# Cosine attention on one core: the order of work on all five engines replaced, the program left as it is

## The chip, the core and the metric

The kernel runs on one core of one Trainium2 chip. The metric is the device time of one execution in microseconds. A core has four compute engines that this kernel uses side by side: TensorE (PE in the profile; it multiplies and transposes), VectorE (DVE), ScalarE (ACT) and GpSimd (POOL); SyncE (SP) issues nearly all transfers. Each engine works through its own list of instructions strictly in order. An instruction that needs a result of another engine waits for a semaphore, and everything behind it on the same engine waits with it.

## The reference

Inputs Q, K and V are 8 x 12 x 512 x 64 floats, tau is 0.1.

```python
Q_norm = Q / (norm(Q, axis=-1) + 1e-10)
K_norm = K / (norm(K, axis=-1) + 1e-10)
scores = einsum('bhqd,bhkd->bhqk', Q_norm, K_norm) / tau
weights = exp(scores - max(scores))
weights = weights / (sum(weights) + 1e-10)
out = einsum('bhqk,bhkd->bhqd', weights, V)
```

Scores lie between -10 and 10, so the kernel leaves the maximum out of the exponent. For 96 heads of 512 x 512 scores that is 25.2 million exponentials.

## The kernel before

**Tiling.** Two heads form a pair, and there are 48 pairs, 0 to 47. Of each pair, 128 partitions hold four query rows (or key rows) each. The work of one pair is a fixed set of operations, which the program names with a kind and the pair's number:

- LD.s.0 and LD.s.1 load Q and K (256 KB each, line 429), LV.s loads V (line 432). SP issues them.
- SQ.s.0 squares Q and K on POOL (line 250). SSQ.s adds the squares in groups on PE (line 268, eight matmuls), and RED.s.0 on DVE sums the rest (line 276).
- NEW.g.0 to NEW.g.7 on DVE turn the sums of a group of one or two pairs into inverse norms, by an integer first guess and two Newton steps (lines 390 to 402). Pairs 0 to 2 take them by a logarithm and an exponential on ACT instead (LN and EX, lines 282 and 286).
- SCL.s.0 (Q, on DVE) and SCL.s.1 (K, mostly on POOL) scale rows to unit length in bf16 (line 296; line 327 for pair 0).
- TR.s transposes both on PE (line 484), EVA.s copies the result out of PSUM on DVE (line 490). For seven pairs K is transposed by a transfer instead, XT.s.1.
- SCO.s.0 to SCO.s.3 are the scores on PE, two matmuls of 512 columns each (line 512; line 359 for pair 0).
- EXP.s.0 to EXP.s.3 are the exponentials on ACT, 128 x 1024 each (line 527; lines 364 and 523 for the first and the last pair).
- VC.s converts V to bf16 on POOL (line 532), beside a column of ones.
- PV.s.h.t multiply weights and V on PE (line 555, four matmuls of 65 columns each); the ones give the sum of the weights. For the last pair they are PV.47.i.c (line 612).
- RCP.s and NRM.s divide on DVE (lines 569 and 571; 626 and 628 for the last pair), ST.s stores (line 575; 632 for the last pair). Of the last pair the output goes in three parts; ACT issues the last store.

**Buffers.** Score banks are two: the scores of a chunk may start once the exponential two chunks earlier has read its bank. Q and K lie in 18 buffers, V in 6 (LV.s waits for VC.(s-6)), squares in 6, the scaled rows and their transposes in 5 each, the weights in 3, outputs in 8. The PSUM banks for transposes, square sums and outputs pass from one user to the next.

**Order.** Nothing is planned when the kernel is built. A table, ORDER, holds one written-out list for each engine, and the program emits each engine's operations in that order:

```python
order = {e: [by_token.pop(t) for t in text.split()] for e, text in ORDER.items()}
```

Waits come from each operation's list of needs; a wait on a semaphore value that the engine has already seen is left out:

```python
for p in o.waits:
    k = id(p.sem)
    if p.val > max(seen.get(k, 0), want.get(k, (None, 0))[1]):
        want[k] = (p.sem, p.val)
```

A list therefore decides two things: when an operation gets its turn, and which operations stand behind it while it waits. The lists hold 200 operations for SP, 143 for POOL, 451 for DVE, 702 for PE and 212 for ACT.

Of the kernel before, what the change touches and what calls it, by code (L numbers as in the profile page):

```python
# [124 lines left out]
def bass_cosine_similarity_attention_kernel(  # L125
# [518 lines left out]
    if FILL[1]:  # L644
# [8 lines left out]
XT = {9: (1,), 15: (1,), 21: (1,), 27: (1,), 33: (1,), 39: (1,), 45: (1,)}  # L653
# [15 lines left out]
        LD.0.0.0 LD.0.0.1 LD.1.0 LD.1.1 LD.2.0 LD.2.1 LD.3.0 LD.3.1 LV.0 LD.4.0 LD.4.1 LD.5.0 LD.5.1 LD.6.0 LV.1  # L669
        LD.6.1 LD.7.0 LD.7.1 LD.9.1 LD.9.0 LV.2 LV.3 LV.5 LD.8.1 LD.8.0 LV.4 LD.13.0 LD.15.0 LV.7 LD.11.1 LD.10.0  # L670
        LD.10.1 LD.11.0 LV.6 LV.8 LD.16.0 LD.14.1 ST.1 LD.12.0 LD.12.1 LD.13.1 LD.15.1 ST.4 XT.9.1 LD.18.0 LV.9
        LD.14.0 LV.10 LD.21.0 ST.0 LD.17.0 LV.14 LV.11 LD.16.1 LD.19.0 ST.5 ST.3 LD.24.0 LD.17.1 ST.2 LV.12 LV.15
        LD.18.1 LD.27.0 ST.6 LD.20.0 LV.13 LD.19.1 LD.23.0 LD.20.1 XT.15.1 LV.17 LV.16 LD.21.1 LD.24.1 LD.23.1 ST.7
        LD.22.0 LD.27.1 LV.20 ST.9 LD.30.0 LD.22.1 LV.21 LV.18 LD.25.0 LD.26.0 ST.8 LV.23 LD.25.1 ST.10 LD.28.0 LV.19
        LD.26.1 LD.29.0 LD.31.0 LD.31.1 LD.28.1 XT.21.1 LD.35.0 ST.11 ST.13 LD.32.0 LV.22 ST.12 LD.35.1 LV.25 ST.14
        LD.40.0 LD.29.1 ST.16 LD.30.1 LV.24 ST.19 LD.33.0 LD.36.0 LD.40.1 ST.15 LD.32.1 LD.33.1 LV.26 LV.27 LD.44.0
        ST.17 LV.28 XT.27.1 ST.20 LD.42.0 ST.23 LV.29 ST.18 LD.39.1 LD.34.1 LD.34.0 LD.37.1 LD.41.0 LV.32 LD.37.0
        LD.42.1 ST.22 LV.33 LD.36.1 LV.31 LV.30 ST.21 LD.39.0 ST.25 LD.38.0 LD.47.0 LV.35 ST.24 LV.34 XT.33.1 LD.38.1
        LV.37 LV.38 ST.28 ST.29 LD.44.1 LV.36 LD.45.1 LD.41.1 LD.43.0 LV.43 LD.46.0 LD.43.1 ST.26 ST.27 LD.45.0 LV.41
        LV.42 LV.44 ST.30 LV.40 ST.33 ST.32 XT.39.1 LV.39 LD.46.1 LD.47.1 ST.31 ST.36 LV.45 ST.37 LV.47 ST.38 ST.34  # L680
# [13 lines left out]
        wz RED.0.0.0 RED.0.1.0 RED.0.1.1 SCL.0.1.0 SCL.0.0.0 RED.0.0.1 EVA.0.1.0 SCL.0.1.1 EVA.0.0.0 SQ.1.1 SCL.0.0.1
        EVA.0.1.1 RED.1.0 EVA.0.0.1 SCL.1.1 SCL.1.0 RED.2.0 EVA.1.1 EVA.1.0 SCL.2.0 SCL.2.1 RED.3.0 NEW.0.0 NEW.0.1
        NEW.0.2 EVA.2 NEW.0.3 NEW.0.4 NEW.0.5 NEW.0.7 NEW.0.6 SCL.3.1 RED.4.0 SCL.3.0 RCP.0 NEW.1.0 NRM.0 RED.5.0
        NEW.1.1 NEW.1.2 NEW.2.0 EVA.3 NEW.1.3 NEW.2.1 NEW.1.4 NEW.2.2 NEW.1.5 NEW.1.6 NEW.1.7 SCL.4.0 RED.6.0 NEW.2.3
        RCP.1 NEW.2.4 NRM.1 RED.7.0 NEW.2.5 NEW.2.6 NEW.3.0 EVA.4 NEW.3.1 SCL.5.0 NEW.2.7 NEW.3.2 RCP.2 NRM.2 RED.9.0
        NEW.3.3 NEW.3.4 EVA.5 NEW.3.5 NEW.3.7 NEW.3.6 SCL.6.0 RCP.3 NRM.3 RED.8.0 NEW.4.0 NEW.4.1 EVA.6 SCL.7.0
        NEW.4.2 NEW.4.3 RCP.4 NEW.4.4 NRM.4 NEW.4.5 NEW.4.6 EVA.7 NEW.4.7 SCL.8.0 RCP.5 NRM.5 RED.10.0 SCL.9.0 EVA.8  # L700
        EVA.9 RED.11.0 NEW.5.0 NEW.5.1 NEW.5.2 RCP.6 NRM.6 NEW.5.3 NEW.5.4 RED.13.0 NEW.5.5 NEW.5.7 NEW.5.6 SCL.10.0
        RCP.7 NRM.7 RED.12.0 SCL.11.0 EVA.10 NEW.6.0 NEW.6.1 NEW.6.2 EVA.11 NEW.6.3 NEW.6.4 NEW.6.5 NEW.6.6 NEW.6.7
        RED.15.0 SCL.12.0 RCP.8 NRM.8 RED.14.0 EVA.12 NEW.7.0 NEW.7.1 NEW.7.2 SCL.13.0 NEW.7.3 RCP.9 NRM.9 NEW.7.4
        RED.16.0 NEW.7.5 NEW.7.7 EVA.13 NEW.7.6 SCL.14.0 RCP.10 NRM.10 RED.17.0 SCL.15.0 EVA.14 NEW.8.0 EVA.15 NEW.8.1
        NEW.8.2 NEW.8.3 NEW.8.4 RCP.11 NRM.11 NEW.8.5 NEW.8.6 SCL.17.0 NEW.8.7 SCL.16.0 RED.18.0 RCP.12 NRM.12
# [26 lines left out]
        SCO.1.1 TR.2 PV.0.0.0 PV.0.0.1 PV.0.0.2 SCO.1.2 PV.0.0.3 PV.0.1.0 SCO.1.3 SSQ.4 SCO.2.0 PV.0.1.1 PV.0.1.2  # L732
# [108 lines left out]
```

## Time and profile before

| | |
|---|---|
| three timed runs | 191.36, 192.54 and 193.3 us, median 192.54 us |
| the profiled execution's own time | 191.03 us |
| its span, first to last instruction | 189.2 us |
| busy: ACT, PE, POOL, DVE | 181.3, 174.0, 160.1, 146.1 us |
| transfers | 51.73 MB, mean 273 GB/s |
| clock granted to PE | 1.0 throughout |

The span is what the views show; the 1.83 us between it and the execution's own time lie around it. Busy time of PE is modelled at the ends of matmuls, so its share says less than ACT's. An idle gap of an engine is put down to what released the instruction behind it, by the time of semaphore events. A row of the timeline or of the chain gives the start in us, the length in us, the engine, the line and the operation; neighbours of the same kind are merged, with a count.

### The profile page before, as it was taken

The numbers are of one execution on the slowest core, as the hardware profiler recorded it, in microseconds if no ns is written. First come the engines' busy times: TensorE is split into PE (matmuls) and PEld (weight loads), VectorE is DVE, ScalarE is ACT, GpSimd is POOL, SyncE is SP. The second block draws the span as 40 slices with busy tenths as digits, with TensorE's granted clock in tenths as the row PEclk, the third lists the DMA queues.
The fourth block names the chain that finished last, engine by engine and source line by source line (L and its number), as shares of the span: only waits on it lengthen the run. The fifth ranks groups of instructions, "written<-read, shape, count | busy, mean of one in ns | idle before, by whom it ended". The sixth has DMA issues, their size and how long they took to land.

```text
span 189.2 us, 7234 instructions
## 1 busy us (share of the span) xinstructions
PE 174.0 (92%) x3023; PEld 110.2 (58%) x3023; DVE 146.1 (77%) x451; ACT 181.3 (96%) x209; POOL 160.1 (85%) x147
## 2 busy tenths in 40 slices
PE   7999998999998999998898999999999999988893
PEld 5455664665665565665565656565656666654542
DVE  2999988879887977878798688876869877697424
ACT  5599999999999999999999999999999999999992
POOL 1599999999999999999999999999899998355100
PEclk9999999999999999999999999999999999999999
DMA  5999999579999999999999999999999570938423
GB/s 151 335 349 349 348 350 368 175 234 310 361 359 251 309 353 346 314 254 349 376 373 303 241 343 299 352 255 281 294 318 328 132 243 22 309 90 170 132 93 116
DMA packets 56257, 51.73 MB, mean 273 GB/s; under 512 B 6944, under 2 KB 56224, under 8 KB 56224
## 3 DMA queue, kind: packets, MB, share of 16 engines
q1 hardware_dynamic: 55792, 50.93, 86.4%
q8 instruction: 24, 0.39, 0.9%
q10 hardware_dynamic: 432, 0.33, 0.6%
q14 instruction: 9, 0.07, 0.1%
HBM read 37.75 MB, written 12.58 MB: 266 GB/s over the span
## 4 chain that ended last, share of the span: by engine, by line
ACT 84%; PE 6%; DVE 4%; POOL 2%; DMA 2%; issue 0%; ACTq 0%; DVEq 0%
ACT et L527 80%; ACT et L523 2%; DMA qk<-in_K_dram 2%; PE bps L268 2%; PE scps L512 1%; POOL qn L296 1%; PE scps L359 1%; POOL sq L250 1%; DVE qt L490 1%; PE bps L555 1%; PE bps L484 1%; DVE qn L296 1%; DVE qn L327 1%; ACT et L364 1%; PE bps L333 0%
## 5 line engine op out<-in xcount | busy, mean ns | idle before, releaser
L527 ACT ACTIVATE et<-scps 128x1024 bf16<-128x1024 f32 x184 | 168.9, 1168 | 0.2 <-PE scps L512 0.2
L250 POOL TENSOR_TENSOR sq<-qk 128x1024 bf16<-128x1024 f32 (+2 forms) x48 | 87.3, 1830 | 6.0 <-DMA qk<-in_Q_dram 5.7
L512 PE MATMUL scps<-qt 64*128 64x512 bf16 x376 | 74.1, 386 | 8.5 <-ACT et L527 7.2
L555 PE MATMUL bps<-vb,et 128*128 128x65 bf16 x1472 | 66.4, 194 | 0.0
L555 PEld LDWEIGHTS bps<-vb,et 128*128 128x128 bf16 x1472 | 51.8, 98 | 24.5 <-issue 16.2
L296 POOL TENSOR_TENSOR qn<-qk,rk 128x512 bf16<-128x512 f32 x44 | 45.3, 1042 | 9.4 <-DVE rk L398 5.7
L490 DVE COPY qt<-bps 128x1024 bf16<-128x1024 bf16 (+1 forms) x46 | 29.9, 650 | 10.9 <-PE bps L484 10.0
L296 DVE TENSOR_TENSOR qn<-qk,nps 128x512 bf16<-128x512 f32 x50 | 33.8, 681 | 0.5
L571 DVE TENSOR_TENSOR ob<-bps,rd 128x512 f32<-128x512 f32 x47 | 32.5, 692 | 1.1
L512 PEld LDWEIGHTS scps<-qt 64*128 64x128 bf16 x376 | 18.3, 93 | 25.9 <-ACT et L527 14.3
L268 PE MATMUL bps<-sq,ident 128*128 128x128 bf16 x376 | 29.1, 220 | 0.5 <-POOL qn L296 0.5
L532 POOL TENSOR_SCALAR vb<-vf 128x512 bf16<-128x512 f32 x48 | 29.5, 625 | 0.0
L268 PEld LDWEIGHTS bps<-sq,ident 128*128 128x128 bf16 x376 | 21.1, 98 | 11.0 <-issue 8.1
L569 DVE RECIPROCAL rd<-bps 128x8 f32<-128x8 f32 x47 | 9.7, 207 | 18.7 <-PE bps L555 15.2
L484 PE MATMUL bps<-ident,qn 64*128 64x64 bf16 x680 | 17.9, 191 | 1.4 <-DVE nps L276 0.3
L484 PEld LDWEIGHTS bps<-ident,qn 64*128 64x128 bf16 x680 | 13.2, 95 | 7.8 <-DVE nps L276 3.4
L276 DVE TENSOR_REDUCE nps<-bps 128x16 f32<-128x128 f32 x45 | 13.4, 297 | 2.1 <-PE bps L268 2.1
L390 DVE TENSOR_TENSOR nps<-nps,ys 128x32 f32<-128x32 f32 (+1 forms) x48 | 9.1, 192 | 1.0
L394 DVE SCALAR_TENSOR_TENSOR nps<-nps,ys 128x32 f32<-128x32 f32 (+1 forms) x48 | 9.1, 191 | 0.7
L237 PE MATMUL scps<-warm_in 128*128 128x256 bf16 x23 | 4.8, 394 | 1.1 <-DVE warm_in L232 1.1
L398 DVE SCALAR_TENSOR_TENSOR nps<-nps,ys 128x16 f32<-128x16 f32 (+1 forms) x25 | 4.3, 177 | 0.5
L402 DVE TENSOR_SCALAR ys<-nps 128x32 int32<-128x32 int32 (+1 forms) x24 | 4.4, 181 | 0.4
(45 smaller groups left out, 46.8 us busy)
## 6 DMA issues: line engine op xcount, KB each, us to landing
vf<-in_V_dram SPq DMA_DIRECT2D x48, 256.0 KB, 5.4
qk<-in_Q_dram SPq DMA_DIRECT2D x47, 256.0 KB, 5.9
qk<-in_K_dram SPq DMA_DIRECT2D x47, 256.0 KB, 6.0
out_dram<-ob SPq DMA_DIRECT2D x47, 256.0 KB, 4.5
qk<-in_Q_dram SPq DMA_DIRECT2D x2, 128.0 KB, 2.6
qk<-in_K_dram ACTq DMA_DIRECT2D x2, 128.0 KB, 2.8
out_dram<-ob SPq DMA_DIRECT2D x1, 128.0 KB, 2.3
qt<-qn SPq DMA_TRANSPOSE x7, 3.5
```

Source lines behind the costliest of these rows:

```text
L250: emit = lambda e: e.tensor_tensor(out=b, in0=a, in1=a, op=ALU.mult)
L268: last = e.matmul(out=ps[:, 0:128], lhsT=ident[:, :], rhs=sq[s % R_SQ][:, :, 8 * k : 8 * k + 8], start=(k == 0), stop=(k == 7))
L276: lambda e: e.tensor_reduce(out=dst(None), in_=ps[:, 0:128].rearrange("p (w g e) -> p w g e", w=2, e=8), axis=AX.X, op=ALU.add))
L296: lambda e: e.tensor_tensor(out=o, in0=x, in1=r, op=ALU.mult))
L484: last = e.transpose(t_ps[:, k, b, :], qn[s % R_QN][ks, b // NT, b % NT].rearrange("p h d -> p (h d)"), ident[ks, ks])
L490: lambda e, lo=lo, hi=hi: e.tensor_copy(out=qt[iqt][:, :].rearrange("p w t (k x) -> p k (w t) x", k=2)[:, :, lo:hi], in_=t_ps[:, :, lo:hi]))
L512: last = e.matmul(out=sc_ps[:, 2 * b + k, :], lhsT=qt[iqt][64 * h : 64 * h + 64, 1, n, :], rhs=qt[iqt][64 * h : 64 * h + 64, 0, :, :], sta ...
L527: lambda e, c=c, b=b: e.activation(out=et[iet][:, c, :, :], in_=sc_ps[:, 2 * b : 2 * b + 2, :], func=ACT.Exp, scale=scale, bias=bias))
L532: lambda e: e.tensor_scalar(out=vb[:, iq, :, :, 0:DIM].rearrange("p c h d -> p h c d"), in0=vf[iv][:, :, :].rearrange("p h (c d) -> p h c ...
L555: last = e.matmul(out=o_ps[:, h, 65 * t : 65 * t + 65], lhsT=et[iet][:, c, h, 128 * t : 128 * t + 128], rhs=vb[:, iq, c, h, :], start=(c = ...
L569: lambda e: e.reciprocal(out=rd[io][:, :], in_=grid[:, :, :, DIM]))
L571: lambda e: e.tensor_tensor(out=ob[io][:, :], in0=grid[:, :, :, 0:DIM], in1=rd[io][:, :].unsqueeze(3).to_broadcast([128, 2, NT, DIM]), op= ...
```

## The change

All five lists are replaced by others over the same operations. No operation is added, removed or given to another engine, and all code outside the table is the same. Of the places in the lists, 175 of 200 hold another operation on SP, 100 of 143 on POOL, 282 of 451 on DVE, 159 of 702 on PE and 4 of 212 on ACT. No operation moves by more than 47 places on SP, 22 on POOL, 11 on DVE, 5 on PE and 1 on ACT. The users of each PSUM bank follow one another as before.

The beginning of DVE's list, and its end:

```diff
-        wz RED.0.0.0 RED.0.1.0 RED.0.1.1 SCL.0.1.0 SCL.0.0.0 RED.0.0.1 EVA.0.1.0 SCL.0.1.1 EVA.0.0.0 SQ.1.1 SCL.0.0.1
-        EVA.0.1.1 RED.1.0 EVA.0.0.1 SCL.1.1 SCL.1.0 RED.2.0 EVA.1.1 EVA.1.0 SCL.2.0 SCL.2.1 RED.3.0 NEW.0.0 NEW.0.1
+        wz RED.0.1.0 RED.0.0.0 RED.0.1.1 RED.0.0.1 SCL.0.1.0 SCL.0.0.0 SCL.0.1.1 EVA.0.1.0 EVA.0.0.0 SQ.1.1 EVA.0.1.1
+        SCL.0.0.1 RED.1.0 EVA.0.0.1 SCL.1.0 SCL.1.1 RED.2.0 EVA.1.0 EVA.1.1 SCL.2.0 SCL.2.1 RED.3.0 NEW.0.0 NEW.0.1
...
-        EVA.47 RCP.45 NRM.45 RCP.46 NRM.46 RCP.47.0 NRM.47.0 RCP.47.1 RCP.47.2 NRM.47.2 NRM.47.1""",
+        RCP.45 NRM.45 RCP.46 NRM.46 RCP.47.0 NRM.47.0 RCP.47.1 NRM.47.1 RCP.47.2 NRM.47.2""",
```

The beginning of ACT's list (the rest is the same):

```diff
-        LD.0.1.0 LD.0.1.1 table SQ.0.0.0 SQ.0.1.0 SQ.0.1.1 LN.0.0 EX.0.0 LN.0.1 EX.0.1 SQ.1.0 EXP.0.0.0 EXP.0.0.1 LN.1
-        EX.1.1 EX.1.0 EXP.0.0.2 EXP.0.1.0 LN.2 EX.2.1 EX.2.0 EXP.0.1.1 EXP.1.0 EXP.1.1 EXP.1.2 EXP.1.3 EXP.2.0 EXP.2.1
+        LD.0.1.0 LD.0.1.1 table SQ.0.1.0 SQ.0.0.0 SQ.0.1.1 LN.0.0 EX.0.0 LN.0.1 EX.0.1 SQ.1.0 EXP.0.0.0 EXP.0.0.1 LN.1
+        EX.1.0 EX.1.1 EXP.0.0.2 EXP.0.1.0 LN.2 EX.2.1 EX.2.0 EXP.0.1.1 EXP.1.0 EXP.1.1 EXP.1.2 EXP.1.3 EXP.2.0 EXP.2.1
```

The beginning of PE's list:

```diff
-        warm.15 warm.16 warm.17 warm.18 TR.0.1.0 TR.0.0.0 fill.0 fill.1 fill.2 fill.3 TR.0.1.1 SCO.0.0.0 SCO.0.0.1
-        SCO.0.0.2 SSQ.1 TR.0.0.1 SCO.0.0.3 SCO.0.1.0 SCO.0.1.1 SSQ.2 TR.1.1 TR.1.0 SCO.0.1.2 SCO.0.1.3 SCO.1.0 SSQ.3
+        warm.15 warm.16 warm.17 warm.18 TR.0.1.0 TR.0.0.0 TR.0.1.1 fill.0 fill.1 fill.2 SCO.0.0.0 SCO.0.0.1 SCO.0.0.2
+        SSQ.1 fill.3 TR.0.0.1 SCO.0.0.3 SCO.0.1.0 SCO.0.1.1 SSQ.2 TR.1.0 TR.1.1 SCO.0.1.2 SCO.0.1.3 SCO.1.0 SSQ.3
```

and three places in its middle. In the first, the old list has six value products between two scores; in the second, the new list has six before SCO.6.0 (PV.4.0.0 to PV.4.0.3 stand just ahead of this line):

```diff
-        PV.12.0.0 PV.12.0.1 SCO.14.2 PV.12.0.2 PV.12.0.3 PV.12.1.0 PV.12.1.1 PV.12.1.2 PV.12.1.3 SCO.14.3 SSQ.19
+        PV.12.0.0 PV.12.0.1 PV.12.0.2 PV.12.0.3 PV.12.1.0 SCO.14.2 PV.12.1.1 PV.12.1.2 PV.12.1.3 SCO.14.3 SSQ.19
...
+        PV.4.1.0 PV.4.1.1 SCO.6.0 PV.4.1.2 PV.4.1.3 SCO.6.1 SCO.6.2 TR.7 PV.5.0.0 PV.5.0.1 PV.5.0.2 SCO.6.3 PV.5.0.3
...
+        SCO.40.2 PV.38.1.1 PV.38.1.2 PV.38.1.3 SSQ.45 SCO.40.3 SCO.41.0 TR.42 PV.39.0.0 PV.39.0.1 SCO.41.1 PV.39.0.2
```

POOL's list is the same for its first 21 operations (SQ.0.0.1 to VC.4); after that the conversions VC mostly stand later and the squares and scalings earlier. Two stretches:

```diff
-        VC.14 SQ.19.0 VC.13 SCL.16.1 VC.15 SQ.20.0 SCL.17.1 SQ.21.0 VC.16 SCL.18.1 SCL.19.1 VC.17 SQ.22.0 SQ.23.0
-        SQ.24.0 SCL.20.1 SCL.21.1 VC.18 SQ.25.0 SQ.26.0 VC.19 SCL.22.1 VC.21 VC.20 SCL.23.1 SQ.27.0 SQ.28.0 SCL.24.1
+        VC.14 SQ.19.0 SCL.16.1 VC.13 SQ.20.0 SCL.17.1 SQ.21.0 VC.15 SCL.18.1 VC.16 SCL.19.1 SQ.22.0 VC.17 SQ.23.0
+        SCL.20.1 VC.18 SCL.21.1 SQ.24.0 VC.20 SQ.25.0 SCL.22.1 VC.19 VC.23 VC.21 SQ.26.0 SCL.23.1 SQ.27.0 SCL.24.1
```

In SP's list, the load of V for pair 20 with what stands around it:

```diff
-        LD.22.0 LD.27.1 LV.20 ST.9 LD.30.0 LD.22.1 LV.21 LV.18 LD.25.0 LD.26.0 ST.8 LV.23 LD.25.1 ST.10 LD.28.0 LV.19
+        LV.19 LD.26.0 LV.17 LD.23.0 LD.23.1 LD.25.0 ST.12 LV.18 ST.11 LD.35.0 LV.23 LD.27.1 LV.20 LD.25.1 LV.22
```

More of the change, by code (lines that the diff above doesn't have):

```diff
@@ new lines @@
+        SCO.1.1 TR.2 PV.0.0.0 PV.0.0.1 SCO.1.2 PV.0.0.2 PV.0.0.3 PV.0.1.0 SCO.1.3 SSQ.4 PV.0.1.1 PV.0.1.2 PV.0.1.3
+        SCO.2.0 SCO.2.1 SSQ.5 PV.1.0.0 SCO.2.2 TR.3 PV.1.0.1 PV.1.0.2 SCO.2.3 PV.1.0.3 PV.1.1.0 PV.1.1.1 SCO.3.0 SSQ.6
+        PV.1.1.2 PV.1.1.3 SCO.3.1 SSQ.7 SCO.3.2 TR.4 SCO.3.3 PV.2.0.0 PV.2.0.1 PV.2.0.2 PV.2.0.3 SCO.4.0 PV.2.1.0
+        PV.2.1.1 PV.2.1.2 PV.2.1.3 SCO.4.1 SSQ.9 SCO.4.2 TR.5 SCO.4.3 PV.3.0.0 PV.3.0.1 PV.3.0.2 PV.3.0.3 SCO.5.0
+        PV.3.1.0 PV.3.1.1 PV.3.1.2 PV.3.1.3 SCO.5.1 SSQ.8 SCO.5.2 TR.6 SCO.5.3 PV.4.0.0 PV.4.0.1 PV.4.0.2 PV.4.0.3
@@ new lines @@
+        SCO.28.1 PV.26.0.0 PV.26.0.1 SCO.28.2 PV.26.0.2 PV.26.0.3 PV.26.1.0 PV.26.1.1 PV.26.1.2 PV.26.1.3 SCO.28.3
+        SSQ.32 SCO.29.0 TR.30 SCO.29.1 PV.27.0.0 PV.27.0.1 PV.27.0.2 PV.27.0.3 SCO.29.2 SSQ.34 SCO.29.3 PV.27.1.0
+        PV.27.1.1 PV.27.1.2 PV.27.1.3 SCO.30.0 SSQ.35 SCO.30.1 PV.28.0.0 PV.28.0.1 TR.31 SCO.30.2 PV.28.0.2 PV.28.0.3
+        SCO.30.3 PV.28.1.0 PV.28.1.1 PV.28.1.2 PV.28.1.3 SCO.31.0 SCO.31.1 TR.32 PV.29.0.0 PV.29.0.1 PV.29.0.2
+        SCO.31.2 PV.29.0.3 PV.29.1.0 PV.29.1.1 PV.29.1.2 PV.29.1.3 SCO.31.3 SSQ.36 SCO.32.0 PV.30.0.0 PV.30.0.1
@@ new lines @@
+        PV.34.0.3 SCO.36.2 PV.34.1.0 PV.34.1.1 PV.34.1.2 PV.34.1.3 SCO.36.3 SSQ.41 SCO.37.0 TR.38 SCO.37.1 PV.35.0.0
+        PV.35.0.1 PV.35.0.2 PV.35.0.3 SCO.37.2 PV.35.1.0 PV.35.1.1 PV.35.1.2 PV.35.1.3 SCO.37.3 SSQ.42 SCO.38.0
+        PV.36.0.0 PV.36.0.1 TR.39 SCO.38.1 PV.36.0.2 PV.36.0.3 PV.36.1.0 PV.36.1.1 PV.36.1.2 PV.36.1.3 SCO.38.2 SSQ.43
+        SCO.38.3 PV.37.0.0 TR.40 SCO.39.0 PV.37.0.1 PV.37.0.2 PV.37.0.3 SCO.39.1 PV.37.1.0 PV.37.1.1 PV.37.1.2
+        PV.37.1.3 SCO.39.2 SSQ.44 SCO.39.3 TR.41 SCO.40.0 PV.38.0.0 PV.38.0.1 PV.38.0.2 PV.38.0.3 SCO.40.1 PV.38.1.0
```

178 lines of the change are left out of this document (81 added, 97 removed).

## The prediction

> **What bounds the kernel now.** I read the page first (busy shares), then the chain of work that ended last in order of time, then the exponentials of line 527 by themselves, then the two ends of the timeline.
>
> ```profile
> span 189.2 us, 7234 instructions
> PE 174.0 (92%) x3023; PEld 110.2 (58%) x3023; DVE 146.1 (77%) x451; ACT 181.3 (96%) x209; POOL 160.1 (85%) x147
> L527 ACT ACTIVATE et<-scps 128x1024 bf16<-128x1024 f32 x184 | 168.9, 1168 | 0.2 <-PE scps L512 0.2
> ```
>
> ACT is busy 96% of the span, and before its 184 large exponentials it sat idle only 0.2 us. No order changes their number. The chain says when they run:
>
> ```profile
> 12.02 1.03 ACT et L364
> ...
> 24.28 1.03 POOL qn L296
> ...
> 27.75 1.01 POOL qn L296
> 28.76 0.03 issue
> 28.79 0.62 PE bps L268 x8
> 29.41 0.34 PE scps L512 x2
> 29.75 0.02 issue
> 29.77 152.28 ACT et L527 x166
> 182.05 3.84 ACT et L523 x5
> ```
>
> From 29.77 to 182.05 ACT runs 166 exponentials without a break. How steady is it? One takes at least 1018 ns by itself:
>
> ```profile
> L527 ACT ACTIVATE et<-scps x184: 1018/1154/1343, 12.9 to 181.0; 128x1024 bf16<-128x1024 f32 x184
> ```
>
> So the step from end to end is (152.28 - 1.02)/165 = 0.917 us. At that step 184 take 184 x 0.917 + 0.10 = 168.8, and the group was busy 168.9 and idle 0.2: **some 0.3 us is lost in the whole middle**. Most of it sits at 29.4 to 29.8, where the chain crosses from POOL through PE to ACT. The median record, 1154 ns, is 136 ns longer than the shortest and the longest 325: an exponential is issued that much ahead of its turn. I read this as slack: scores may come 0.14 to 0.3 us late at no cost. This stretch of PE bears it out:
>
> ```profile
> 62.02 0.39 PE L512 MATMUL scps<-qt 64*128 64x512 bf16 x2 [0.18 <-ACT et L527]
> 62.34 0.91 PE L555 MATMUL bps<-vb,et 128*128 128x65 bf16 x24
> 63.19 0.39 PE L512 MATMUL scps<-qt 64*128 64x512 bf16 x2
> ```
>
> Six value products between two score pairs put the second 1.17 us after the first, 0.25 more than the step, inside the unbroken run of 166. What an order can still win is therefore the head (before 12.94), the crossing near 29, and the tail (after 182.05 + 3.84 = 185.89).
>
> **The change part by part.** No instruction is added or removed, and no wait: every needed result is the same, only the place in five queues differs.
>
> *Head.* Rows of ACT and DVE, and the landing of pair 1's K load, issued at 2.17:
>
> ```profile
> 3.35 1.25 ACT L248 ACTIVATE sq<-qk 128x256 bf16<-128x256 f32 x3 [0.35 <-DMA qk<-in_Q_dram]
> 4.58 0.21 ACT L282 ACTIVATE xl<-xs 128x8 f32<-128x8 f32 x1
> 6.15 0.21 ACT L282 ACTIVATE xl<-xs 128x8 f32<-128x8 f32 x1 [1.15 <-DVE xs L318]
> 7.84 1.08 ACT L364 ACTIVATE et<-scps 128x512 bf16<-128x512 f32 x2 [0.58 <-PE scps L359]
> 9.15 0.22 ACT L282 ACTIVATE xl<-xs 128x16 f32<-128x16 f32 x1 [0.23 <-DVE xs L276]
> 7.32 0.69 DVE L250 TENSOR_TENSOR sq<-qk 128x512 bf16<-128x512 f32 x1
> qk<-in_K_dram SPq DMA_DIRECT2D x1, 256.0 KB, 5.1
> 11.38 0.60 PE L359 MATMUL scps<-qt 64*128 64x512 bf16 x2
> ```
>
> DVE now sums the last squares of pair 0 (RED.0.0.1) before scaling head 0, so the logarithm that waited 1.15 us starts some 0.7 us earlier, near 5.4. On the other side K's square now goes ahead of Q's on ACT. The wait of 0.35 ended when Q's half landed; if K's lands with it or up to 0.2 later (both were issued at 0.79), Q's square ends one step of 0.3 later and the first logarithm moves from 4.58 to about 4.8, head 0's scaling by 0.3. The third scaling then needs no wait, and head 0's scores come at about 7.1 instead of 7.42: the wait of 0.58 shrinks by 0.3. But the gain dies at the next step. DVE squares pair 1's K at 7.32, when it lands (2.17 + 5.1 = 7.27); that square, its sums on PE, their reduction and LN.1 move little. I get LN.1 at 9.03 (was 9.15) and the next exponential 0.1 earlier. Pair 1's Q is then scaled and transposed first, so the last scores of pair 0 (row at 11.38) come about 0.09 earlier, and the first exponential of pair 1 starts at 12.86 instead of 12.94. Head: -0.08 us; ends 0 (landings gate all) and -0.3 (all of the 0.58 wait's share kept).
>
> *The crossing near 29.* POOL's order is the same up to 28.8 us (SQ.2.0 to VC.4), and it is back to back from
>
> ```profile
> 10.38 1.89 POOL L250 TENSOR_TENSOR sq<-qk 128x1024 bf16<-128x1024 f32 x1 [0.22 <-DMA qk<-in_K_dram]
> 28.79 0.62 PE L268 MATMUL bps<-sq,ident 128*128 128x128 bf16 x8 [0.47 <-POOL qn L296]
> ```
>
> So nothing on POOL moves before 28.76, and if PE's square sums SSQ.8 are again released there, EXP.5.2 again starts at 29.77, and whatever the head and the stretch before won is spent waiting. By the program SSQ.8 needs only SQ.8.0, which the chain shows ending at 27.75; PE was free at about 28.3 and still started 27 ns after the POOL instruction behind it. I can't say why. Ends: 0 if it recurs; if it doesn't, the head's 0.08, the 0.07 of a smaller stall near 21.2 and about 0.26 here are won, -0.4. I take 0, the profile's own attribution.
>
> The rival reading is a pause for code. The page shows that stream:
>
> ```profile
> q8 instruction: 24, 0.39, 0.9%
> ```
>
> 24 blocks of 16 KB, and 0.47 us of PE idle at only one of them that no wait explains. [...]
>
> *Middle, 30 to 182.* SQ and SCL move ahead of the V conversions on POOL (0.6 us each), which frees time where TR.13, TR.14 or SSQ.17 were close; worth nothing, since no exponential waited there. On PE six value products stand between two scores at new places (before SCO.6.0, SCO.28.3, SCO.41.2) and no longer at SCO.14.3, SCO.31.3 and SCO.33.3: an even trade. The fullest new stretch is before SCO.40.3: three products (0.12 each by the 0.78 us that six took above), eight sums (0.55, as 28.79 to 29.34) and the score's own 0.32 are 1.23 us, 0.31 over the step, so 0 to 0.2 beyond the slack. DVE moves by at most 11 places, with 23% idle. I take +0.05, ends 0 and +0.3.
>
> SP's queue changes most (175 of 200 places): loads still run many pairs ahead, transposes stand at the same ranks within three. The exception is a rival below.
>
> *Tail.*
>
> ```profile
> 185.99 1.34 SPq L632 DMA_DIRECT2D out_dram<-ob  x2
> 186.47 0.29 DVE L628 TENSOR_TENSOR ob<-scps,rd 128x128 f32<-128x128 f32 x1
> 186.68 0.28 DVE L628 TENSOR_TENSOR ob<-bps,rd 128x128 f32<-128x128 f32 x1
> out_dram<-ob ACTq DMA_DIRECT2D x1, 64.0 KB, 1.7
> out_dram<-ob SPq DMA_DIRECT2D x1, 64.0 KB, 1.7
> ```
>
> Before, DVE divided the last quarter first, and the other quarter's store was issued at 186.99 and landed at 188.7, last of all. Now NRM.47.1 goes at about 186.1 and its store as soon as SP is through with the one before, 186.67, landing 188.4. NRM.47.2 follows 0.02 later than now, stored by ACT at 186.81, landing 188.5. Tail: -0.17, if the span closes on the last landing; ends 0 and -0.3.
>
> Sum: 0 (head, spent at the crossing) + 0 + 0.05 - 0.17 = -0.1. Span 189.1. The profiled execution took 191.03, 1.83 around its span; it would take 190.9. The three timed runs have the median 192.54, 1.5 above it, so I forecast **192.4**. The runs lie between 191.36 and 193.3, so about 1% is what a measurement of this kernel can tell from no change.
>
> **The rivals.**
>
> *A: the crossing opens.* For: SSQ.8's own input was there 1 us earlier. Against: the release within 0.03 us of a POOL end. All the gains count: -0.08 - 0.07 - 0.26 - 0.17 + 0.05 = -0.5, **192.0**.
>
> *B, slower: V loads issued just in time.* POOL now converts V of pair 20 five places earlier than before, after SQ.24.0. Before, it was the second conversion in the row at 86.20, so it began near 86.8; the work taken out from ahead of it is SQ.25, SQ.26, SCL.22.1, VC.19 and VC.21, 1.87 + 1.87 + 1.04 + 0.63 + 0.63 = 6.0 us, so it wants to start near 80.8. Its load LV.20 stands in SP's queue two places behind LV.23, which waits for VC.17 to free its buffer:
>
> ```profile
> 72.16 0.63 POOL L532 TENSOR_SCALAR vb<-vf 128x512 bf16<-128x512 f32 x1
> 80.89 3.75 POOL L250 TENSOR_TENSOR sq<-qk 128x1024 bf16<-128x1024 f32 x2
> 86.20 1.21 POOL L532 TENSOR_SCALAR vb<-vf 128x512 bf16<-128x512 f32 x2
> 84.34 0.62 PE L268 MATMUL bps<-sq,ident 128*128 128x128 bf16 x8
> vf<-in_V_dram SPq DMA_DIRECT2D x1, 256.0 KB, 3.9
> vf<-in_V_dram SPq DMA_DIRECT2D x1, 256.0 KB, 6.3
> ```
>
> VC.17 ended at 72.79 and now comes behind one square (1.85), at 74.6; LV.20 is issued near 75.7. V loads landed 3.9 us after issue at 72.8 and 6.3 at 64.2. At 3.9 it lands at 79.6 and costs nothing. At 6.3 it lands at 82.0, 1.3 late, and POOL stands. The square SQ.25.0 ended 1.56 before PE took it (80.89 + half of 3.75 against 84.34) and is 0.6 later already, so 1.3 - 0.95 - 0.14 of slack = 0.2 reaches ACT, and with K's load behind it (0.75) about 1.0. It decides from a landing 5 us after issue. The same pattern stands at VC.26 and VC.40, where loads have some 6.4 us: one place +0.2 to 1.0, three places up to 3. Against: SP has just waited for VC.17, so its queue is short, as it was at 72.8. With +0.9, **193.3**; with all three, 195.4.
>
> *C: no difference at all*, the tail not closing on the landing: 192.5.
>
> **How the numbers follow.** Forecast with C 0.50 (C 0.08 of it), A 0.25, B 0.25. Range: down to A less half the spread of the runs (192.0 - 1.0 = 191.0), up to B with half of its further part (194.3). Faster by over 1% (below 190.6) needs more than every gain found: 0.05, for what I missed. Slower by over 1% (above 194.5) needs B at two or three places: 0.13. Within 1%: 0.82.
>
> **What the changed profile would show.** Step of 0.917 unchanged; a run of some 166 exponentials again starting at 29.77 (A: 29.3 to 29.4); the second logarithm without its wait of 1.15 and LN.1 near 9.0; the last store's landing near 188.5. B would show POOL idle before L532, released by the V load, near 80, 91 or 140, and a break in that run. A step other than 0.917, or an idle of ACT over 0.5 us anywhere after 30, would make the prediction wrong.

## The result, and the profile after

The changed kernel is slower by 0.7%: 193.95 us median (192.12 to 195.54) against 191.85 us (191.28 to 193.3) for the kernel before, 12 runs each; ratio 1.0069, 95% interval 1.0040 to 1.0097. The forecast was 192.4, a tenth of a microsecond below the median known then (192.54).

The twelve times come in two groups: five from 192.12 to 192.47, with a mean granted TensorE clock of 0.997 to 1.0, and six from 193.93 to 194.15, with 0.987 to 0.991 (the last, 195.54, stands apart; such runs are left out of the ratios). The profiled execution, 194.15 us with a span of 192.3, is of the second group. Its page, in the lines that answer to those shown of before:

```profile
span 192.3 us, 7235 instructions
...
PE 175.9 (91%) x3023; PEld 111.3 (58%) x3023; DVE 146.2 (76%) x451; ACT 181.6 (94%) x209; POOL 160.3 (83%) x147
...
PEclk9999996999999999999999999999999999999998
...
q8 instruction: 24, 0.39, 0.9%
...
L527 ACT ACTIVATE et<-scps 128x1024 bf16<-128x1024 f32 x184 | 169.2, 1156 | 2.8 <-PE scps L512 2.6
```

The busy time of the 184 exponentials is as before (169.2 against 168.9), but ACT now stood idle 2.8 us ahead of them instead of 0.2, and in the seventh of the 40 slices, 29 to 34 us, PE's clock is down. The chain of work that ended last says where (start, length, what):

```profile
28.32 0.32 PE scps L512
28.64 1.57 issue
30.21 0.39 PE scps L512
30.60 0.97 PE bps L268 x8
31.56 0.54 PE scps L512
32.10 0.47 PE bps L484 x16
32.57 0.43 PE scps L512 x2
32.99 1.27 PE bps L555 x24
34.26 0.34 PE scps L512 x2
34.60 0.02 issue
34.63 149.53 ACT et L527 x163
```

PE ran the first product of the score pair SCO.5.1, stood for 1.57 us while it waited for nothing that the profile shows, and ran the second. From 34.63 on, 163 exponentials follow without a break at (149.53 - 1.02)/162 = 0.917 us, the old step. So all of the loss in the middle is over by 34.6 us; what is left lies at the two ends. Counted from end to end of neighbouring exponentials, what exceeds the step is 1.72 at EXP.5.1, 0.60 at EXP.5.2 and 0.65 at EXP.6.0, 2.97 together; before, this place lost 0.26, at EXP.5.2.

Why the second and third came late too, the stretches of the same kernel show (from and to, length, busy time and count of PE, PEld, DVE, ACT, POOL, then granted clock, DMA share, GB/s):

```profile
23.68:27.09 3.41, 3.34 (x69) 2.11 (x66) 3.02 (x11) 3.41 (x5) 2.60 (x4) 1.00 1.11 349
27.09:30.50 3.41, 1.81 (x28) 0.94 (x24) 2.03 (x7) 1.93 (x3) 3.41 (x5) 1.00 1.07 338
30.50:33.92 3.42, 3.42 (x48) 2.38 (x48) 1.77 (x6) 2.80 (x3) 3.33 (x3) 0.50 0.62 188
33.92:37.33 3.41, 2.96 (x62) 1.84 (x60) 2.59 (x10) 2.87 (x4) 0.71 (x1) 1.00 0.93 273
```

For 3.41 us just after the pause TensorE was granted half its clock; PE was busy without a gap and late. The sum closes: head +0.10, EXP.2.0 to EXP.3.2 +0.23, this place 2.97 - 0.26 = 2.71, from the end of the last exponential to the end of the span 3.40 against 3.32, +0.08: 3.1, the difference of the spans (192.3 - 189.2).

**A reason.** I take the 24 packets of the q8 row, 16,384 bytes each, for blocks of PE's program. In the trace of the kernel before, PE has 3023 weight loads, 3023 products, 67 semaphore instructions and 2 drains, together 6,115, over 24 blocks 255 a block; I took 256. I let the blocks begin at program places 191, 447, 703 and so on, because with this offset a block is fetched as PE crosses the boundary ahead of it, where the DMA engines are less busy (before: fetched at 177.02, crossed at 176.93, share 0.52; 185.04 and 185.12, share 0.23). By this count the block from 703 is asked for when PE crosses 447, inside SSQ.7 near 21.3 us (no event marks the asking; the time is read off the count, to some 0.2 us), and 703 lies between the two products of SCO.5.1 (places 701 to 704). Before, two instructions apart, it lay right behind SCO.5.1 (699 to 702), on the first instruction of SSQ.8: the very matmul whose wait the profile of before put down to POOL. The DMA row of the changed kernel for 27.50 to 28.62 us (packets, MB, share), then its K loads issued from 21 to 31:

```profile
q8 instruction: 1, 0.02, 6.1%
```

```profile
qk<-in_K_dram SPq DMA_DIRECT2D x2, 256.0 KB, 7.1
```

Between 21.30 and 27.50 no such packet appears; it ran from 27.53 to 28.61. Its end lies 7.2 us after the crossing at 21.40, as long as a load issued then takes to land (7.1). I call this theory **code**. Its rivals: **semaphore** (SSQ.8 is released by POOL, as the prediction took it) and **orders** (the new orders of loads, PE, DVE or POOL lose the time by themselves).

### The profile page after: what moved, and what is told of

The parts are those of the page before. It is cut to its first block, busy times and chain, and to the rows that moved or that the text cites. A ratio compares the mean times of both kernels' runs of the same rounds, so it can differ in the third digit from the quotient of the medians.

```text
span 192.3 us, 7235 instructions
## 1 busy us (share of the span) xinstructions
PE 175.9 (91%) x3023; PEld 111.3 (58%) x3023; DVE 146.2 (76%) x451; ACT 181.6 (94%) x209; POOL 160.3 (83%) x147
## 4 chain that ended last, share of the span: by engine, by line
ACT 80%; PE 12%; DVE 3%; DMA 1%; issue 1%
ACT et L527 80%; PE scps L512 4%; PE bps L555 2%; PE bps L268 2%; DMA qk<-in_K_dram 1%; PE scps L359 1%; PE bps L484 1%; PE bps L333 1%; PE bps L543 1%; DVE xs L318 1%; ACT et L364 1%; DVE ob L628 1%; DVE qt L490 0%; DVE ob L571 0%; PE nps L612 0%
## 5 line engine op out<-in xcount | busy, mean ns | idle before, releaser
L527 ACT ACTIVATE et<-scps 128x1024 bf16<-128x1024 f32 x184 | 169.2, 1156 | 2.8 <-PE scps L512 2.6
L512 PE MATMUL scps<-qt 64*128 64x512 bf16 x376 | 75.0, 388 | 9.8 <-ACT et L527 6.6
L268 PE MATMUL bps<-sq,ident 128*128 128x128 bf16 x376 | 29.7, 222 | 0.1
L364 ACT ACTIVATE et<-scps 128x1024 bf16<-128x1024 f32 (+1 forms) x5 | 4.0, 851 | 1.3 <-PE scps L359 1.1
```

The source lines that it names most:

```text
L268: last = e.matmul(out=ps[:, 0:128], lhsT=ident[:, :], rhs=sq[s % R_SQ][:, :, 8 * k : 8 * k + 8], start=(k == 0), stop=(k == 7))
L512: last = e.matmul(out=sc_ps[:, 2 * b + k, :], lhsT=qt[iqt][64 * h : 64 * h + 64, 1, n, :], rhs=qt[iqt][64 * h : 64 * h + 64, 0, :, :], sta ...
L527: lambda e, c=c, b=b: e.activation(out=et[iet][:, c, :, :], in_=sc_ps[:, 2 * b : 2 * b + 2, :], func=ACT.Exp, scale=scale, bias=bias))
```

## The experiments

Each ratio is against runs of the kernel before that were taken beside it (their medians lie between 191.54 and 192.09), and it isn't the quotient of two medians; the times given are medians.

### Fewer loads ahead of the block

SP is held: ST.0 and ST.1 move ahead in SP's queue. ST.0 is issued at 17.6 to 18.2 us, ST.1 waits for NRM.1 at 21.9, and so no load is issued from about 17 to 22. On the kernel before:

```diff
-  LD.8.1 LD.8.0 LV.4 LD.13.0 ... LD.14.1 ST.1 LD.12.0 ... LD.21.0 ST.0 LD.17.0
+  LD.8.1 LD.8.0 LV.4 ST.0 ST.1 LD.13.0 ... LD.14.1 LD.12.0 ... LD.21.0 LD.17.0
```

> The kernel before with the same two stores moved ahead to stand behind LV.4, so SP issues no load from about 17 to 21.9 us. Theory 'code': the 0.47 us for which PE stood before SSQ.8 at 28.79 was also a block of code (asked for at 21.15, landed at 27.49), and the end of POOL's instruction 27 ns earlier was chance. SSQ.8 then starts at about 28.3, EXP.5.2 has no wait, and the exponentials run without a break from near 21 to 182: 0.26 us less, ratio 0.998 to 0.9995. Theory 'semaphore' (what I took in the prediction: SSQ.8 is released by a POOL instruction at 28.76): POOL's order is unchanged, SSQ.8 starts within 0.05 us of the end of that POOL instruction, wherever that falls, and the time is 1.000.

Measured: 191.40 us, ratio 0.9967 (0.9936 to 0.9997). PE, then POOL, in time order, then the chain:

```profile
28.34 0.39 PE L512 MATMUL scps<-qt 64*128 64x512 bf16 x2
28.67 0.62 PE L268 MATMUL bps<-sq,ident 128*128 128x128 bf16 x8
```

```profile
28.11 1.04 POOL L296 TENSOR_TENSOR qn<-qk,rk 128x512 bf16<-128x512 f32 x1
```

```profile
13.46 168.74 ACT et L527 x184
```

The block landed at 25.43, and SSQ.8 began right behind SCO.5.1, while the POOL instruction that should have released it still had 0.48 us to run. *Semaphore* falls. All 184 exponentials form one run. The time fell by more than was expected, and this profile doesn't show why: EXP.1.0 began at 13.35, 0.41 later than before, and its span is 189.5 against 189.2, so the gain rests on the twelve runs.

On the changed kernel, with the same two stores behind LD.8.1:

```diff
-  LD.8.0 LD.10.0 LD.8.1 LD.11.1 ... LD.15.0 XT.9.1 ST.0 ST.1 LD.16.1
+  LD.8.0 LD.10.0 LD.8.1 ST.0 ST.1 LD.11.1 ... LD.15.0 XT.9.1 LD.16.1
```

> The changed kernel with two stores of SP's queue, ST.0 and ST.1, moved ahead to stand behind LD.8.1; they wait for NRM.1 (21.94 us), so SP issues no load from about 16 to 22 us. Theory 'code': the 1.57 us for which PE stood between the two matmuls of SCO.5.1 was the block of PE's own instructions, asked for at 21.25 us behind ten loads in flight and landed at 28.61. With the loads in flight down to one or two at 21.25, the block lands by 24, PE doesn't stand near 28.2, the granted clock stays at 1.0 there, the 3.0 us that ACT lost on EXP.5.1, EXP.5.2 and EXP.6.0 fall to under 0.3, and the span is 189.2 to 189.6 instead of 192.3; ratio to the kernel before 0.996 to 1.002 instead of 1.007. Theory 'orders' (the new orders of POOL, DVE and PE lose the time themselves, by a release of POOL as I took it in the prediction): those orders are as in the changed kernel, so the loss of about 3 us in the span stays, or grows by what the later loads cost.

Measured: 191.74 us, ratio 0.9986 (0.9954 to 1.0018): the loss is gone with DVE, PE, ACT and POOL in the new orders. But the block still landed only at 27.51, not by 24, though only three loads and ST.0 were in flight at the crossing and all four had landed by 24.14. A load issued at 22.55, 1 us after the crossing, landed at 25.55, before the block's packet began at 26.55. So the block doesn't simply stand behind the loads that are ahead of it. PE's pause in SCO.5.1 was 0.19 us:

```profile
28.22 0.39 PE L512 MATMUL scps<-qt 64*128 64x512 bf16 x1
28.80 0.39 PE L512 MATMUL scps<-qt 64*128 64x512 bf16 x1 [0.19 <-issue]
```

The hold also made later transfers late (EXP.21.0 waited 0.5 us for the transpose XT.21.1). An attempt to mend that, with XT.9.1 ahead of nine loads that are used late:

```diff
-  ST.0 ST.1 LD.11.1 LD.13.0 LV.4 LD.15.1 LV.5 LD.10.1 ... LD.15.0 XT.9.1 LD.16.1
+  ST.0 ST.1 LV.4 LV.5 LD.10.1 LV.6 LD.11.1 ... LV.7 XT.9.1 LV.8 LD.14.0 ... LD.16.0 LD.16.1
```

> The changed kernel with SP held as in e3_after_hold (ST.0 and ST.1 behind LD.8.1), and the loads behind them sorted by when they are used, with XT.9.1 ahead of nine of them (in e3_after_hold it was issued behind them, landed at 42.80 and held up EXP.9.0 by 0.17 us, the loads behind it EXP.10.2 by 0.16). If the block's lateness is all that the new orders cost, nothing of the 3.0 us near 30 us is left and the time is that of the kernel before with the same hold: ratio 0.995 to 0.999. If the new orders cost something of their own beside it: 1.000 to 1.004.

Measured: 193.32 us, ratio 1.0086 (1.0055 to 1.0117, seven runs), against both expectations, and without a pause at SCO.5.1. PE's waits name the cause:

```profile
PE bps L555 <- POOL vb L532: 0.9, 1, 0.9
PE scps L512 <- DMA qt<-qn: 0.9, 1, 0.9
```

At 51.78 the products of pair 9 waited for a V conversion and at 66.08 SCO.15.0 for its transpose: SP stood at XT.9.1 and the loads behind it came late. This is rival B's mechanism, made by my own edit; it says nothing on the change.

On the held kernel before, one more wait lets pair 1's loads go first:

```diff
-  [key(n, s - R_QK, *y) for n in ("SCL", "SQ") for y in ...],
+  [key(n, s - R_QK, *y) for n in ("SCL", "SQ") for y in ...] + ([("LD", 0, 0, 1)] if (s, w) == (2, 0) else []),
```

> The kernel before with SP held as in e5_before_hold, and with one wait more in the head: LD.2.0 is issued only when LD.0.0.1 has landed (3.94 us, instead of 2.68). In the traces pair 1's K load lands between 6.97 and 8.22, beside the loads behind it, and the first exponential of pair 1 starts 5.6 to 5.9 us later. If those loads take bandwidth from it, LD.1.1 lands at 5.8 to 6.5, LN.1 and EXP.1.0 start 0.4 to 0.8 us earlier, ratio 0.993 to 0.996. If the loads are served in the order of their issue, LD.1.1 lands as before, the later loads come about 1 us later, and the ratio is 0.997 to 1.001.

Measured: 191.59 us, ratio 1.0000 (0.9976 to 1.0024). LD.1.1 landed at 6.54 and EXP.1.0 began at 12.84, 0.1 earlier than before and 0.5 earlier than with the hold alone (13.35), but the loads behind came later: V of pair 6 landed at 34.41 (33.08 with the hold alone), and behind its conversion on POOL a scaling for which PE stood 1.16 us at 36.7 (TR.8). This profile is of the slowest of the twelve runs (193.63 us).

### One queue at a time

The first 37 places of SP's queue exchanged, the rest of each kernel as it was:

```diff
-  LV.0 LD.4.0 LD.4.1 ... LV.3 LV.5 LD.8.1 LD.8.0 LV.4 LD.13.0 LD.15.0 ...
+  LD.4.1 LV.0 LD.4.0 ... LV.3 LD.8.0 LD.10.0 LD.8.1 LD.11.1 LD.13.0 LV.4 ...
```

> The kernel before, with the first 37 places of SP's queue as in the changed kernel (the loads up to LD.11.0) and the rest in its own order; the other four queues are those of before. If the order of the loads is what made the block land 1.1 us later (28.61 against 27.49), PE stands some 1.6 us near 28.3 to 30, the clock drops to a half behind it, and the ratio is 1.007 to 1.012. If the block's landing depends on where PE asks for it and on the number of loads in flight alone, the block is asked for at 21.15 with nine or ten in flight as now, and the ratio is 0.999 to 1.002.

> The other way round: the changed kernel with the first 37 places of SP's queue as in the kernel before. If the order of the loads makes the block late: PE stands about 0.5 us at SCO.5.1, the clock stays at 1.0, ACT loses about 0.5 instead of 3.0 us, ratio 0.998 to 1.002. If the other four queues carry the loss: 1.005 to 1.010, as the changed kernel.

Measured: old kernel with new loads 192.11 us, 0.9999 (0.9971 to 1.0027); new kernel with old loads 193.94 us, 1.0086 (1.0046 to 1.0127), six of ten runs at a clock of 0.987 to 0.991. The order of these first loads isn't it. (The profile of the second is of a run without the loss: block asked for at 22.34, landed 26.51, no pause. Its times spread as the changed kernel's do.) In the profile of the first, SSQ.8 again started late, at 29.13, and the POOL instruction that the profile names had ended 0.10 us earlier, not 0.03: one more sign that it isn't the releaser.

The changed kernel with PE's first 117 operations, or DVE's first 94, in the old order:

```diff
- (PE) PV.2.1.3 ... PV.3.0.3 SCO.5.0 PV.3.1.0 ... PV.4.1.1 SCO.6.0 ...
+ (PE) PV.2.1.3 ... PV.3.0.3 PV.3.1.0 SCO.5.0 ... SCO.6.0 PV.4.1.0 ...
- (DVE) RED.0.1.1 RED.0.0.1 SCL.0.1.0 SCL.0.0.0 SCL.0.1.1 ...
+ (DVE) RED.0.1.1 SCL.0.1.0 SCL.0.0.0 RED.0.0.1 EVA.0.1.0 ...
```

> The changed kernel with PE's queue up to SCO.6.3 (117 operations, to about 34 us) in the order of the kernel before. The block boundary then falls behind SCO.5.1 (program places 699 to 702, boundary at 703), as in the kernel before, and no longer between its two matmuls. If PE's order, and with it the place of the boundary, is what makes PE stand 1.6 us and the clock fall to a half, this is back at 0.998 to 1.003, with a mean granted clock of 0.995 or more in nearly all runs. If the other queues carry the loss, 1.005 to 1.010, with about half of the runs at a clock of 0.987 to 0.991, as the changed kernel and as the changed kernel with the old loads.

> The changed kernel with DVE's queue up to NRM.5 (94 operations) in the order of the kernel before; the boundary stays between the two matmuls of SCO.5.1. If DVE's order makes the loss (later releases of PE before 28 us), 0.998 to 1.003. If the block's arrival against PE's place does, 1.005 to 1.010 with about half of the runs at a clock of 0.987 to 0.991.

Measured: with the old PE order 192.38 us, 1.0042 (1.0000 to 1.0083), one of ten runs below 0.995, no pause in the profile; between the two expectations. (In that profile EXP.1.0 began at 13.84, 0.8 us later than in the changed kernel.) With the old DVE order 196.23 us, 1.0185 (1.0107 to 1.0263), in only four runs, and in the profiled one for another reason:

```profile
4.40:7.81 3.41, 1.41 (x15) 0.85 (x14) 3.08 (x9) 1.60 (x6) 1.49 (x4) 1.00 0.99 302
7.81:11.22 3.41, 3.41 (x19) 1.62 (x18) 1.51 (x4) 1.09 (x2) 3.09 (x3) 0.50 1.09 369
```

DVE's old order against PE's new one left PE busy 1.41 of 3.41 us in the head, and half the clock was granted from 7.81 to 18.05: EXP.1.0 began at 17.42 instead of 13.04. Whether the other three runs lost their time so isn't shown (clocks 0.970, 0.998 and 0.998). The run decides nothing about 28 us.

### The same orders, the boundary elsewhere

The warm-up matmuls at the head of PE's list only fill time. One more or fewer shifts every later instruction by two places in the program. Where there are more of them, their columns are cut so that the row takes as long; one fewer is left at 256 columns, a row 0.2 us shorter (19 took 4.23 us). The four fillers before the first scores come from the same code, so their columns are cut too.

```diff
-WARM = 19    # rhs 256 columns
+WARM = 20    # rhs 243 columns, on the kernel before: boundary into SCO.5.1
+WARM = 18    # 256 columns, on the changed kernel: boundary behind SCO.5.1
```

> The kernel before with 20 warm-up matmuls of 243 columns in place of 19 of 256, so that PE's program is two instructions longer ahead of everything and nothing else changes. The boundary at 703 falls between the two matmuls of SCO.5.1 (places 701 to 704), as in the changed kernel. Theory 'code': the pause of PE moves from before SSQ.8 to the middle of SCO.5.1, the score pair of EXP.5.1. The block is asked for two instructions earlier, by which it can't come sooner than 0.05 us, so the time of its arrival is as before; by the order of work behind it EXP.5.2 ends some 0.3 us later than now, ratio 1.000 to 1.003; if the place of the pause also decides over the clock, 1.005 to 1.010 with half of the runs at 0.987 to 0.991. Theory 'semaphore': SSQ.8 waits on POOL as before, SCO.5.1 is whole, 1.000.

> The changed kernel with 18 warm-up matmuls in place of 19, PE's program two instructions shorter. The boundary falls behind SCO.5.1, as in the kernel before. Theory 'code': SCO.5.1 runs whole at about 28.3 and PE's pause, if there is one, stands before SSQ.8, wherever POOL is. If the two instructions decide over the loss, ratio 0.998 to 1.003 and clocks of 0.995 or more; if they only move the pause, 1.005 to 1.010.

Measured: the kernel before with one matmul more takes 192.53 us, 1.0038 (1.0003 to 1.0073). The pause moved into SCO.5.1, as the count says, and was 1.38 us; two of the ten runs had a clock of 0.987 to 0.991:

```profile
28.07 0.39 PE L512 MATMUL scps<-qt 64*128 64x512 bf16 x1
29.83 0.39 PE L512 MATMUL scps<-qt 64*128 64x512 bf16 x1 [1.38 <-issue]
```

The changed kernel with one fewer takes 193.32 us, 1.0048 (1.0015 to 1.0080): the pause moved out of SCO.5.1 to SSQ.8, and the loss didn't go.

```profile
31.56 0.39 PE L512 MATMUL scps<-qt 64*128 64x512 bf16 x2
32.71 0.62 PE L268 MATMUL bps<-sq,ident 128*128 128x128 bf16 x8 [0.75 <-POOL qn L296]
```

(In this profiled run the head took 3.3 us longer, so only the places compare.) Again the profile names POOL; that instruction had ended 0.20 us earlier (31.47 + 1.04 = 32.51). So two instructions decide which operation stands, not whether it does.

Larger shifts on the changed kernel, and one on the kernel before:

```diff
-WARM = 19    # 256 columns
+WARM = 23    # 211 columns: 8 instructions, changed kernel
+WARM = 27    # 180 columns: 16 instructions, changed kernel; kernel before
```

> The changed kernel with 27 warm-up matmuls of 180 columns in place of 19 of 256: PE's program is 16 instructions longer ahead of everything. The boundaries fall 16 instructions earlier: the block is asked for between PV.1.1.2 and PV.1.1.3 (20.7 us, was 21.4), and its first instruction lies in PV.3.1.2 (27.9 us). Theory 'code': a pause, if the block is late, stands inside PV.3.1.2 and nowhere else near; the block is asked for 0.7 us earlier and needed 0.5 us earlier, so the pause is about as long (1 to 1.6 us), its end 0.3 to 0.7 us earlier; ratio 1.002 to 1.007. Theory 'orders': SCO.5.1 is where PE stands, as in the changed kernel, 1.007.

> The changed kernel with 23 warm-up matmuls of 211 columns: half of the shift of e4_after_shift, 8 instructions. The block is asked for at about 21.0 us (21.40 in the changed kernel, 20.90 in e4_after_shift) and first needed inside PV.3.1.3. If the loss hangs on how many loads are ahead of the block when it is asked for (ten at 21.40, five at 20.90), the ratio lies with e4_after_shift, 0.999 to 1.003, when five or six are ahead in the profile, and with the changed kernel, 1.005 to 1.009, when nine or ten are. If the warm-up row is what helps, half of the help: 1.003 to 1.005 with the block as late as in the changed kernel.

> The kernel before with 27 warm-up matmuls of 180 columns in place of 19 of 256: its program is 16 instructions longer ahead of everything, as in e4_after_shift, and the five orders are its own. The block is asked for at about 20.6 us (was 21.3) and first needed inside PV.3.1.2. Theory 'code': it lands by 25 us as in e4_after_shift (24.86), PE doesn't stand near 28, EXP.5.2 loses its 0.26 us, ratio 0.997 to 0.9995; the changed orders, at the same shift 1.0009, are then 0.1 to 0.4% slower or the same. If the shift helps the changed kernel by something else (the longer row of warm-up matmuls), the pause before SSQ.8 stays at its place, 28.3 to 28.8, ratio 1.000.

Measured: the changed kernel shifted by 16 takes 191.86 us, **1.0009 (0.9982 to 1.0035)**, no run of ten at a clock below 0.995; shifted by 8, 192.27 us, 1.0013 (0.9985 to 1.0041). All five orders are those of the changed kernel, whose own interval begins at 1.0040. The shorter fillers didn't bring this: EXP.1.0 began at 13.13 and 13.16 (13.04 unshifted). In the profile of the shift by 8 the place still cost ACT 1.06 us (0.92 at EXP.5.1, 0.14 at EXP.6.0), so this trace doesn't explain its ratio near 1. The chain of the first:

```profile
13.24 167.81 ACT et L527 x183
```

The kernel before, shifted by 16, takes 191.83 us, 1.0026 (0.9993 to 1.0059): against the expectation not faster: its block landed at 27.15 and not by 25, and four of its twelve runs had a clock of 0.982 to 0.991, which only four of 107 runs of the kernel before had. It isn't apart from the changed one at the same shift. So a shift by itself isn't a cure. PE of the changed kernel shifted by 8, then of the kernel before shifted by 16:

```profile
27.54 0.57 PE L555 MATMUL bps<-vb,et 128*128 128x65 bf16 x13
29.08 0.27 PE L555 MATMUL bps<-vb,et 128*128 128x65 bf16 x3 [0.97 <-issue]
```

```profile
27.59 0.36 PE L555 MATMUL bps<-vb,et 128*128 128x65 bf16 x6
28.58 0.36 PE L555 MATMUL bps<-vb,et 128*128 128x65 bf16 x6 [0.63 <-issue]
```

The first product behind the pause is the second of PV.3.1.3's four, and the third of PV.3.1.2's: place 703 both times. The crossing of 447, the packet's end and the time at which PE goes on, in ten profiles:

| kernel | asked | landed | PE goes on | pause, in |
|---|---|---|---|---|
| before | 21.30 | 27.49 | 28.79 | 0.47, ahead of SSQ.8 |
| changed | 21.40 | 28.61 | 30.21 | 1.57, SCO.5.1 |
| before, shift 2 | 21.36 | 28.37 | 29.83 | 1.38, SCO.5.1 |
| changed, shift 8 | 21.06 | 27.70 | 29.08 | 0.97, PV.3.1.3 |
| before, shift 16 | 20.74 | 27.15 | 28.58 | 0.63, PV.3.1.2 |
| before, new loads | 21.60 | 27.62 | 29.13 | 0.50, ahead of SSQ.8 |
| changed, shift -2 | 24.9 | 31.33 | 32.71 | 0.75, ahead of SSQ.8 |
| changed, held | 21.53 | 27.51 | 28.80 | 0.19, SCO.5.1 |
| before, held | 21.71 | 25.43 | | none |
| changed, shift 16 | 20.90 | 24.86 | | none |

Wherever PE stood, it went on 1.3 to 1.6 us after the packet's end. In the other five profiles it didn't stand, and there it reached place 703 at least 1.2 us after the landing. The block ahead lasts 7.0 us (21.40 to 28.4), so by this estimate a block that lands more than about 5.5 us after it is asked for stops PE.

**What stays open.** Eight to ten transfers were in flight at the crossing wherever SP wasn't held, but between four and ten of them landed before the block did; the shift by 8 had nine in flight and a ratio of 1.0013, so their number doesn't set the loss, as its expectation supposed. What sets the landing, I can't tell. Only one of the changed kernel's twelve runs was profiled, so it isn't shown either that its other slow runs had this pause. Shown is that the pause is PE's wait for its code, that it cost this run 2.7 us with the half clock behind it, and that the loss went, over ten and twelve runs, with the boundary 16 instructions away and with SP held.

## Why the prediction was wrong, step by step

**The crossing near 29** is the step that failed: the sum has it at 0, a wait for POOL that recurs. The prediction noted that SSQ.8's input had been there for 1 us, wrote "I can't say why", took the attribution to POOL, and bounded the place by 0 and -0.4. The releaser that the profile names was the last event before the start, by chance 27 ns ahead; with the block early, SSQ.8 runs through the same POOL instruction. The reading that was right, a pause for code, stood in the text as a rival with only one of 24 blocks to show for it, and the sum took the profile's attribution instead. It should have been priced: two more instructions ahead of SCO.5.1 put the same pause into a score pair, and its length isn't fixed (0.47 us before; 0.19 to 1.57 in the table). Measured in place of 0: +2.7 us in the profiled run, of which 1.72 is the pause and 1.25 the half clock behind it, less the 0.26 of before. The bounds of this term had no end above 0.

**ACT's step** of 0.917 us and **the middle** were right: after 34.63 nothing stands but 0.10 at EXP.47.1, as before.

**The head** had the wrong sign: EXP.1.0 at 13.04, forecast 12.86, was 12.94. ACT in time order, then a line of the chain:

```profile
4.91 0.21 ACT L282 ACTIVATE xl<-xs 128x8 f32<-128x8 f32 x1 [0.20 <-DVE xs L318]
...
5.56 0.21 ACT L282 ACTIVATE xl<-xs 128x8 f32<-128x8 f32 x1 [0.23 <-DVE xs L318]
...
7.81 1.08 ACT L364 ACTIVATE et<-scps 128x512 bf16<-128x512 f32 x2 [1.13 <-PE scps L359]
9.12 0.22 ACT L282 ACTIVATE xl<-xs 128x16 f32<-128x16 f32 x1 [0.23 <-DVE xs L276]
```

```profile
6.99 0.43 PE scps L237 x3
```

The second logarithm lost its wait of 1.15 as said, and LN.1 came at 9.12 (said 9.03). But K's half landed later than the 0.2 us allowed (ACT's squares began at 3.68, 0.33 later than before), so the first logarithm came at 4.91, not 4.8, and three fillers of line 237 now stand on the chain from 6.99 to 7.42, ahead of the first scores: these come at 7.39, not 7.1. A fourth stands ahead of SCO.0.0.3 (9.24, was 9.06), which the prediction didn't follow.

**The tail**: -0.17 forecast, +0.08 measured.

```profile
189.01 1.47 SPq L632 DMA_DIRECT2D out_dram<-ob  x2
```

The issue of ST.47.0 alone took 0.92 us on SP (0.64 before), so ST.47.1 was issued at 189.98, 1.08 behind the last exponential; before it was 186.99, 1.11 behind. In this run the swap won nothing because SP, not DVE, was last. In the changed kernel shifted by 16 that issue took 0.35 us and nothing was won either: ACT's store landed last, 3.05 us behind the last exponential (before, the last landing came 2.80 behind it).

**The rivals.** A didn't happen, though its premise (the release isn't POOL's) was true. B didn't happen: no break after 34.63. What happened was none of the four cases. That 193.95 lies inside the range of 191.0 to 194.3, and the change within 1%, is luck: the upper part of the range was there for B. "An idle of ACT over 0.5 us anywhere after 30" did show the prediction wrong: 1.61 us that ended at 30.63, and 0.54 that ended at 34.63.

## What to carry to other kernels

Where an engine stands with all its inputs there, count its instructions to the next boundary of a code block (every 256 in this program, by the count above) before believing the named releaser, and price a change of order by what operation it puts on the boundary. With the DMA engines busy throughout (share 1.10, 348 GB/s from 21.40 to 28.60 us of the changed kernel), the block landed 7.2 us after the crossing that by the count asks for it, and a load 7.1 us after its issue. Two stores moved ahead took the changed kernel from 1.0069 to 0.9986, a shift of the program by 16 instructions to 1.0009; the same shift gave the kernel before nothing (1.0026), so such a remedy has to be tried on the kernel at hand. The best ratio of this study is that of the kernel before with its two stores moved ahead (0.9967), and its interval ends at 0.9997.

## What the runs showed of the hardware

In the kernel before, where the DMA engines were busy 52% and 23% of the time (176.9 to 178.3 and 185.0 to 186.3 us), the fetch of a block of PE's code began within 0.1 us of the counted crossing of the boundary ahead of it, and the block landed 1.3 and 1.1 us after that; the block asked for at place 447 landed 3.7 to 7.2 us after the crossing (the table's ten profiles; DMA share 1.10 in the changed kernel). In the changed kernel PE stood at one of the 24 boundaries, for 1.57 us; beside the other 23 its matmuls follow one another with at most 0.10 us between them.

The granted clock changed only at steps of 3.41 us (in the changed kernel, whose first record of the full clock is at 6.61, at 30.50 = 6.61 + 7 x 3.413, at 33.92, and at 190.93 = 33.92 + 46 x 3.413), and in the three profiles with a fall near 8, 30 and 40 us PE had been busy for only 1.41, 1.81 and 2.16 us of the stretch before (columns as above):

```profile
26.23:29.64 3.41, 2.22 (x39) 1.33 (x35) 2.65 (x7) 2.56 (x3) 3.41 (x4) 1.00 1.10 351
29.64:33.06 3.42, 3.15 (x59) 1.97 (x60) 2.10 (x7) 2.81 (x4) 3.42 (x4) 1.00 1.09 376
```

```profile
36.51:39.92 3.41, 2.16 (x46) 1.26 (x44) 1.71 (x4) 2.52 (x4) 3.41 (x4) 1.00 0.99 202
39.92:43.33 3.41, 3.34 (x32) 2.20 (x33) 1.60 (x6) 2.22 (x4) 3.41 (x3) 0.50 0.86 274
```

The first pair is the kernel before with shift 2: its pause of 1.38 us was cut by a step at 29.64 (5.75 + 7 x 3.413), PE was busy 2.22 us in the first part, and the clock stayed. The second is the held kernel with one wait more: 2.16 busy, and the clock was halved. With 1.81 (changed kernel) and 1.41 (old DVE order) it was halved too. But busy time alone doesn't decide: in the kernel before with the new loads, a stretch with 2.15 us busy (3.76 to 7.17) left the clock at full, and with the old DVE order it stayed at half through two stretches of 3.41 us busy. The steps begin at another moment in each run (the first record of the full clock stands between 3.8 and 6.8 us in 14 of the 15 profiles), and I suppose from these profiles that the same pause halves the clock in some runs and not in others. As an estimate, if every run had the pause of 1.57 us and the steps fell at random, it would lie within one step in (3.41 - 1.57)/3.41 = 54% of cases; six of the changed kernel's twelve runs had the low clock. That this makes its two groups of times fits, but was not tried by itself; the groups could as well be runs with the pause and runs without.
